# A plain 272-column v unit with the gates in it, and one gate preparation for prompt and sample, in a hybrid attention and mLSTM layer on one Trainium2 core

## The chip, the cores and the metric

The program runs on one core of one Trainium2 chip. Its time is the device time of that core in microseconds, from one execution to the next within some 0.1% here. TensorE is called PE in the profile (its weight loads PEld), VectorE DVE, ScalarE ACT, GpSimd POOL; SP is the engine whose queue issues most DMAs.

## What is computed

One encoder layer for a prompt of 1024 tokens and a sample of 256, with 2048 channels, all in float32. A normalised input is multiplied by one matrix of 9232 columns; its parts feed a neighbourhood attention of 8 heads and a two-way mLSTM of 4 heads, and their gated results go through an output matrix. Of the 9232 columns the last 16 are the mLSTM's gates.

```python
hn = rmsnorm(x, norm_w)
proj = jnp.einsum('btd,dp->btp', hn, w_in)
na_q, na_k, na_v, na_g, ml_qk, ml_v, ml_o, ml_z, ml_gp = jnp.split(proj, cuts, axis=-1)
att = neighbourhood_attention(na_q, na_k, na_v, na_rpb) * jax.nn.silu(na_g)
gates = ml_gp.reshape(B, T, 2, 2, ML_HEADS) + gate_b
log_i = gates[:, :, :, 0]
log_f = jax.nn.log_sigmoid(gates[:, :, :, 1])
...
mixed = jnp.concatenate([att, mem], axis=-1)
return x + jnp.einsum('btm,md->btd', mixed, w_out)
```

## The kernel before

**Numbers in two parts.** Every float32 operand of a large product is split into a high and a low part (`split`, lines 176 to 182, and `split_a`, 184 to 186): ACT rounds the source to the high part, DVE subtracts it from the source for the low part. A product then takes three matmuls: high by high, high by low, low by high (`mm_c`, lines 285 to 287).

**Two stages of projections.** The 1280 tokens (prompt, then sample) are cut into a first group of 768 (GA) and a second of 512 (GB). The first stage makes all columns for the first group, the second stage the same columns for the second group; then come attention and mLSTM units, interleaved, and the output product.

**A pair unit of the first stage** (`pair_a`, from line 484; its tiles are named A with the number of its first 128-column block) makes two blocks of 128 columns for 768 tokens. It treats the product as one of 2 x 2 blocks (column blocks by token halves of 384, contracted over two channel halves) and uses seven block products in place of eight. The sums of the input that this needs are made once, in `first_tiles` (lines 329 to 335), and are held in SBUF as `xb` and `xg` (`xop`, lines 279 to 283): with x(h, t) for channel half h and token half t, operand 1 is x(0,0), 2 is x(1,0), 3 is x(1,1), 7 is x(1,1) - x(0,1). The sums of weights are made on POOL per unit (line 536). Weights are stationary, 384 tokens are moving. For each of four row groups and each of seven products there are one split and six matmuls of 384 columns, 168 matmuls in all. Seven PSUM banks hold the products, three under the tag "pr" (three slots) and four under "a" (five slots). In the last row group DVE folds the banks into the two result tiles (`fold`, lines 501 to 521; additions at line 499, scaling at line 264), which lie in the five slots of "pc".

**What follows a unit** is a generator (`finish_a`, lines 439 to 482) that is stepped on inside the next unit: convolution for the mLSTM's q and k (blocks 24 to 39), storing k or q, a tanh and a store for the output gates (blocks 40 to 47). A v unit (block 56 and up) has its result transposed by PE, two 128 x 128 transposes for each of six token tiles (line 475), then split and stored (`store_v`, lines 234 to 248); tiles 1 and 3 use a "pc" slot for that, the others a single buffer "vo".

**The gates of the first group** (`gates_a`, lines 572 to 607) run behind the second unit (A6). The 16 columns' high and low weights stand side by side as 32 columns of a stationary operand, padded to 128 (tiles gAt), over the same input operands; 64 matmuls of 384 columns (gAb, line 596) make them, and twelve small matmuls (line 604) add high and low and turn them to token-major; DVE adds the bias (line 605) into `gt`.

**The order of units** is a list (lines 620 to 623): 4, 6, 24, 56, 8, 10, 26, 58, 12, 14 and so on, to 54. The loop at line 632 runs it.

**The second stage** begins at line 1475: `proj_v(4)` (token-major, x stationary, 272 columns moving, the gates' 16 among them; matmuls at line 774), the sums of squares, then the gate preparation `ml_gates` (lines 962 to 1088), first for the prompt and then for the sample, with high priority; then `proj_v(0)`, `proj_pair(0)`, and the units `pair_s` (tiles named S). `ml_gates` takes log f, makes running sums with five triangle or ones matrices on PE (line 988), transposes log f and i apart, one token tile at a time (line 1008), copies them out (1009), scans them on DVE in both directions (1015, 1017), and transposes back. The prompt and the sample each have their own scratch tile ("gm", two slots, one of which holds the triangles).

**The order on an engine** is not that of the text. The framework plans it with a model of the engines when the program is built: an instruction has a priority by its place in the text, or a higher one (`tc.high_priority()`), and is placed when its operands and a buffer slot are ready in the model. `tc.issue_after` pins an instruction behind another. On the chip each engine then keeps the planned order.

## Time and profile before

| | us |
|---|---|
| median of 3 runs | 2547.41 |
| lowest and highest | 2546.06, 2548.14 |
| the profiled execution, its own time | 2548.95 |
| its span, first to last instruction | 2547.2 |
| PE busy in the span | 2530.2 |
| DVE, ACT, POOL busy | 1979.9, 1348.7, 597.9 |
| the gates' matmuls of the first group, start to the next unit | 137.35 to 149.35 |
| unit A56 | 179.84 to 208.97 |
| gate preparation, first to last matmul | 1133.17 to 1190.59 |

A row of the profile names the line of the kernel, the engine, the operation, and the tiles written and read ("out<-in", buffer numbers left out). In a row of one tile or line the three figures are the shortest, median and longest duration in ns, then the first and the last start in us. A row of waits gives who waited for whom, the sum in us, the number of times and the longest. A row of the timeline gives start, length and the number of instructions merged. Matmuls overlap, so the distance of their starts and not their duration says how fast they go.

### The profile page before, as it was taken

What the parts mean: (1) busy time and instruction counts of PE and PEld (TensorE: products, weight loads), DVE (VectorE), ACT (ScalarE), POOL (GpSimd) and SP (SyncE); (2) the same over time, 40 slices, a digit from 0 to 9 for tenths busy, and PEclk for the clock granted to TensorE, in tenths of its full rate; (3) what the DMA queues carried; (4) which work ended last, traced back from release to release, by engine and by line L of the source; (5) the groups of instructions that cost most, each with busy time, mean ns of one, the idle gap of its engine ahead of it and who ended that gap; (6) DMA issues with size and microseconds to landing.
All of it is one profiled execution on the core that took longest, in us unless ns stands there. A gap on an engine that the chain in (4) does not pass through costs nothing.

```text
span 2547.2 us, 44847 instructions
## 1 busy us (share of the span) xinstructions
PE 2530.2 (99%) x15165; PEld 2370.7 (93%) x15165; DVE 1979.9 (78%) x4050; ACT 1348.7 (53%) x3053; POOL 597.9 (23%) x895
## 2 busy tenths in 40 slices
PE   9999999999999999999999999999999999999998
PEld 9999999999999999999999899899998888888887
DVE  8868788898969798988875676776775665889696
ACT  8635545444444444465655665666665553344445
POOL 0535555444444444410000011010100103000002
PEclk9999999999999999999999999999999999999999
DMA  6556474536434343476778878888877849646227
GB/s 217 164 159 204 137 231 129 182 120 194 131 112 127 108 129 100 135 245 211 232 247 272 267 267 288 273 261 266 298 230 240 291 126 352 204 145 212 90 87 256
DMA packets 307757, 505.67 MB, mean 199 GB/s; under 512 B 48992, under 2 KB 195080, under 8 KB 307528
## 3 DMA queue, kind: packets, MB, share of 16 engines
q1 hardware_dynamic: 304424, 490.75, 60.0%
q0 software_dynamic: 2960, 11.80, 1.2%
q8 instruction: 120, 1.97, 0.3%
q14 instruction: 109, 0.89, 0.1%
q10 hardware_dynamic: 144, 0.26, 0.0%
HBM read 374.18 MB, written 128.52 MB: 197 GB/s over the span
## 4 chain that ended last, share of the span: by engine, by line
PE 84%; DMA 2%; DVE 1%; issue 0%; ACT 0%; SPq 0%; POOLq 0%; POOL 0%; ACTq 0%; DVEq 0%
PE pc L691 16%; PE po L1681 15%; PE pv L774 6%; PE A40b L287 1%; PE A16b L287 1%; PE A52b L287 1%; PE A48b L287 1%; PE A44b L287 1%; PE A20b L287 1%; PE A42b L287 1%; PE A22b L287 1%; PE A14b L287 1%; PE A38b L287 1%; PE A50b L287 1%; PE A68b L287 1%; PE A46b L287 1%
## 5 line engine op out<-in xcount | busy, mean ns | idle before, releaser
L1681 PE MATMUL po<-wo,mo 128*128 128x512 f32 (+1 forms) x1620 | 374.2, 392 | 0.0
L1681 PEld LDWEIGHTS po<-wo,mo 128*128 128x128 f32 x1620 | 303.5, 188 | 70.0
L179 DVE TENSOR_TENSOR ws<-wr,ws 128x512 fp32r<-128x512 f32 x144 | 98.5, 693 | 38.4 <-ACT ws L178 37.9
L178 ACT CAST ws<-wr 128x512 fp32r<-128x512 f32 x144 | 87.6, 617 | 65.7 <-PE pc L691 58.0
L178 ACT CAST mo<-mb 128x640 fp32r<-128x640 f32 x72 | 52.0, 727 | 110.0 <-PE po L1681 99.5
L119 POOL TENSOR_SCALAR rs<-rs 128x1 f32<-128x1 f32 x9 | 4.2, 468 | 370.0 <-DVE rs L1634 366.9
L179 DVE TENSOR_TENSOR mo<-mb,mo 128x640 fp32r<-128x640 f32 x72 | 58.9, 826 | 30.8 <-ACT mo L178 30.8
L1602 DVE TENSOR_TENSOR y<-y,po 128x512 f32<-128x512 f32 x89 | 57.3, 685 | 13.9 <-PE po L1681 13.7
L178 ACT CAST mo<-ms 128x640 fp32r<-128x640 f32 x40 | 28.9, 725 | 51.2 <-PE po L1681 30.8
L179 DVE TENSOR_TENSOR wsv<-wr_v,wsv 128x512 fp32r<-128x512 f32 x64 | 44.3, 698 | 13.2 <-ACT wsv L178 13.0
L178 ACT CAST wsv<-wr_v 128x512 fp32r<-128x512 f32 x64 | 38.9, 616 | 23.7 <-PE pv L774 12.6
L429 DVE SCALAR_TENSOR_TENSOR pcv<-pco,cw_sb,pcv 128x516 f32<-128x516 f32 x48 | 36.8, 767 | 7.0 <-ACT pcv L423 7.0
L179 DVE TENSOR_TENSOR mo<-ms,mo 128x640 fp32r<-128x640 f32 x40 | 32.9, 821 | 10.0 <-ACT mo L178 10.0
L1616 ACT ACTIVATE jk<-y 128x512 f32<-128x512 f32 x39 | 24.5, 629 | 27.1 <-DVE y L1602 26.8
L1115 POOL MEMSET mls_0v<- 128x2 f32 x4 | 0.4, 101 | 160.4 <-DVE S_dt.float L179 136.9
L132 ACT ACTIVATE xq<-xq 128x1024 f32<-128x1024 f32 x20 | 21.2, 1061 | 31.4 <-DMA xq<-in_xtok_dram 29.0
L287 PE MATMUL fb<-xg,fw 128*128 128x384 f32 x192 | 34.7, 335 | 0.1
L287 PEld LDWEIGHTS fb<-xg,fw 128*128 128x128 f32 x192 | 33.3, 188 | 0.4 <-ACT xg L185 0.4
L1565 DVE TENSOR_TENSOR ms<-mb,mb 128x640 f32<-128x640 f32 x40 | 32.8, 821 | 0.0
L264 DVE TENSOR_TENSOR pco<-pc,rstdb 128x512 f32<-128x512 f32 x28 | 19.1, 687 | 16.6 <-PE pc L691 15.7
L812 DVE CUSTOM_DVE_ANT_0 nap_0st<-nap_0s,nap_0bt 128x384 f32<-128x384 f32 x32 | 17.7, 553 | 15.7 <-PE nap_0s L807 7.8
L815 ACT ACTIVATE nap_0st<-nap_0st,nap_0sm 128x384 f32<-128x384 f32 x32 | 19.7, 617 | 19.0 <-DVE nap_0sm L812 19.0
(2790 smaller groups left out, 8524.1 us busy)
## 6 DMA issues: line engine op xcount, KB each, us to landing
wr<-in_w_in_dram SPq DMA_DIRECT2D x72, 512.0 KB, 4.9
wr_v<-in_w_in_dram SPq DMA_DIRECT2D x32, 512.0 KB, 5.5
wb<-in_w_o_dram SPq DMA_DIRECT2D x48, 256.0 KB, 3.9
xq<-in_xtok_dram SPq DMA_DIRECT2D x20, 512.0 KB, 5.0
mb<-mx POOLq DMA_DIRECT2D x32, 320.0 KB, 7.9
y<-in_xtok_dram SPq DMA_DIRECT2D x35, 256.0 KB, 5.1
wr_wp<-in_w_o_dram SPq DMA_DIRECT2D x16, 512.0 KB, 6.2
vS<-vo SPq DMA_DIRECT2D x24, 256.0 KB, 5.1
```

Source lines behind the costliest of these rows:

```text
L132: S.activation(raw, raw, AF.Square, accum_out=ssq[g][:, t, q : q + 1])
L178: S.copy(hi, src)
L179: return V.tensor_tensor(lo, src, f(hi), op=ALU.subtract)
L287: PE.matmul(o, w(a_), x(b_), start=first and m == 0, stop=last and m == 2)
L429: V.scalar_tensor_tensor(dst[:, a:n], src[:, a + j - pad : n + j - pad], cw_sb[:, ct, j : j + 1], dst[:, a:n], op0=ALU.mult, op1=ALU.add,)
L691: PE.matmul(pb[j], t[j][:, wi, c : c + P], xs[xi], start=first and m == 0, stop=last and m == 2,)
L774: PE.matmul(outs[tt], xs[:, tt * P : (tt + 1) * P], t[:, wi, q * w : (q + 1) * w], start=first and m == 0 and (gates or tt % 2 == 0), stop ...
L815: S.activation(st, st, AF.Exp, bias=sm[:, 0:1], scale=-1.0, accum_out=sm[:, 2:3])
L1565: V.tensor_tensor(t, x, y_, op=op)
L1602: V.tensor_tensor(Y[p, q, tt], Y[p, q, tt], bk, op=op)
L1616: S.activation(jk, Y[p, q, tt], AF.Square, accum_out=ss[t][:, c : c + 1])
L1681: PE.matmul(bk[tt] if o is None else o, m[xi][:, tt * P : (tt + 1) * P], w[wi][:, cs], start=first and kk == 0 and j == 0, stop=last and j ...
```

## The change

`pair_a(56)` and `gates_a` go. In their place stands `unit_vg`, at the sixth place of the order, behind units 8 and 40, which move ahead of it. It makes the 256 v columns and the 16 gate columns together, token-major: the input operands 1, 2, 3 and 7 are stationary, 272 columns of weights are moving. The first token half is x(0,0) a + x(1,0) b, the second is x(1,1)(a + b) - (x(1,1) - x(0,1)) a, with a and b the two channel halves of the weights; eight products in place of seven and no folding afterwards. There are 8 steps of 4 products, 3 token tiles and 3 passes. Six banks hold the results, the three "a" banks those of the first half and the three "pr" banks those of the second. They are scaled, split and stored straight from PSUM, without transposes, and the gates are read from columns 256 to 271 of the same banks. Weights come from a new array, `w_vg`, laid out on the host.

`ml_gates` is cut in two: `ml_gates_all` does log f, the triangle products and the sums bd and bo once for all ten token tiles, and puts i and log f side by side into one tile `mgrw` of 40 columns; `ml_gates` keeps the scans for prompt and sample apart, and transposes both rows at once from `mgrw`.

```diff
--- before.py
+++ after.py
@@ -53,6 +53,7 @@
     xtok: bass.AP,
     w_in: bass.AP,
     w_g: bass.AP,
+    w_vg: bass.AP,
     w_o: bass.AP,
     lnw: bass.AP,
     rpb_tab: bass.AP,
@@ -481,6 +482,43 @@
                 store_v((n1 - NCH) // 2, tt * P, vo, b[:, :256])
                 yield
 
+    def unit_vg(bg):
+        banks = {(z, tt): bank("a" if z else "pr", f"vg{z}{tt}")[:, :272] for z in range(2) for tt in range(3)}
+        for kk in range(8):
+            raw = wa.tile([P, 1024], F32, tag="ra", name=f"vgr{kk}", bufs=NRA)
+            DM.dma_start(raw[:, :544], w_vg[kk])
+            a, b = raw[:, 0:272], raw[:, 272:544]
+            ab = raw[:, 544:816]
+            G.tensor_tensor(ab, a, b, op=ALU.add)
+            for i, z, src, scale in ((1, 0, a, None), (2, 0, b, None), (3, 1, ab, None), (7, 1, a, -1.0)):
+                t = wa.tile([P, GA], F32R, tag="pc", name=f"vgs{kk}{i}", bufs=NPC)
+                t = t[:, :544].rearrange("p (h c) -> p h c", h=2)
+                last_split["ins"] = split(t[:, 0], t[:, 1], src, scale).ins
+                for tt in range(3):
+                    for m, (xi, wi) in enumerate(((0, 0), (0, 1), (1, 0))):
+                        PE.matmul(
+                            banks[z, tt], xop(i, kk, xi)[:, tt * P : (tt + 1) * P], t[:, wi],
+                            start=kk == 0 and i in (1, 3) and m == 0,
+                            stop=kk == 7 and i in (2, 7) and m == 2,
+                        )
+                if i in (2, 7):
+                    next(bg, None)
+        for _ in bg:
+            pass
+        for z, tt in banks:
+            k = 3 * z + tt
+            rc = rcs[0][:, k : k + 1]
+            if k % 2:
+                vo = wa.tile([P, GA], F32R, tag="pc", name=f"vgo{k}", bufs=NPC)
+                vo = vo[:, :512].rearrange("p (a d) -> p a d", a=2)
+            else:
+                vo = wa.tile([P, 2, 256], F32R, tag="vo", name=f"vgo{k}", bufs=1)
+            store_v(0, k * P, vo, banks[z, tt][:, :256], rc)
+            V.scalar_tensor_tensor(
+                gt[:, k, :], banks[z, tt][:, 256:], rc, gb_sb, op0=ALU.mult, op1=ALU.add
+            )
+        return iter(())
+
     def pair_a(n1, bg=iter(()), hook=None, first=False, pinned=False):
         nm = f"A{n1}"
         tags = ("pr", "pr", "pr", "a", "a", "a", "a")
@@ -569,43 +607,6 @@
             pass
         return finish_a(n1, Cn)
 
-    def gates_a():
...
     opening = first_tiles()
     next(opening)
     cw_sb = const.tile([P, 16, 5], F32, tag="cw", name="cw_sb")
@@ -618,9 +619,10 @@
     DM.dma_start(w4_sb, mlnw)
     V.tensor_scalar(w4_sb, w4_sb, 0.25, None, op0=ALU.mult)
     order = [4, 6]
-    rest = list(range(KT0, QK0, 2)) + list(range(OT0, NCH, 2))
+    rest = [KT0, OT0, *range(KT0 + 2, QK0, 2), *range(OT0 + 2, NCH, 2)]
     for i in range(NU):
         order += [QK0 + 2 * i, NCH + 2 * i, *rest[2 * i : 2 * i + 2]]
+    order[3:6] = [KT0, OT0, NCH]
     pools = []
 
     def second_pools():
@@ -630,9 +632,10 @@
 
     bg = opening
     for i, n1 in enumerate(order):
-        bg = pair_a(n1, bg, second_pools if i == len(order) - 1 else None, i == 0, i == 1)
-        if i == 1:
-            gates_a()
+        if n1 == NCH:
+            bg = unit_vg(bg)
+        else:
+            bg = pair_a(n1, bg, second_pools if i == len(order) - 1 else None, i == 0, i == 1)
         k = i - 4
         if 0 <= k < 8:
             x_square(1, k)
@@ -959,34 +962,33 @@
             for i, (cm, base) in enumerate(((-1, 0), (1, 0), (1, -1), (-1, -1)))
         ]
 
-    def ml_gates(sq, tris):
-        nt, t0 = (2, 8) if sq == "s" else (8, 0)
-        T = nt * P
-        nm = f"mg{sq}"
-        ig = gt[:, t0 : t0 + nt, 0:8]
-        fg = gt[:, t0 : t0 + nt, 8:16]
+    def ml_gates_all(tris):
+        n = TT // P
+        ig, fg = gt[:, :, 0:8], gt[:, :, 8:16]
 
         def sm(name):
-            return late.tile([P, nt, 8], F32, tag=f"{nm}{name}", name=f"{nm}{name}")
-
-        bd, bo, em = (sm(n) for n in ("bd", "bo", "em"))
-        tmp = xs2.tile([P, 512], F32, tag="gm", name=f"{nm}tmp", bufs=2)
-        lf, e, PL, EX, tot, mc, a1, mF = (
-            tmp[:, i * nt * 8 : (i + 1) * nt * 8].rearrange("p (t c) -> p t c", c=8)
-            for i in range(8)
+            return late.tile([P, n, 8], F32, tag=f"mg{name}", name=f"mg{name}")
+
+        bd, bo, em = (sm(x) for x in ("bd", "bo", "em"))
+        tmp = xs2.tile([P, 512], F32, tag="gm", name="mgtmp", bufs=2)
+        e, PL, EX, tot = (
+            tmp[:, i * n * 8 : (i + 1) * n * 8].rearrange("p (t c) -> p t c", c=8) for i in range(4)
         )
-        mL = e
+        rw = po("mgrw")[:, : n * 40].rearrange("p (t c) -> p t c", c=40)
+        G.memset(rw, 0.0)
+        lf = tmp[:, 4 * n * 8 : 5 * n * 8].rearrange("p (t c) -> p t c", c=8)
         V.scalar_tensor_tensor(e, fg, -1.0, fg, op0=ALU.mult, op1=ALU.max)
         S.activation(e, e, AF.Exp, scale=-1.0)
         S.activation(e, e, AF.Ln, bias=1.0)
         V.tensor_scalar(lf, fg, 0.0, None, op0=ALU.min)
         V.tensor_tensor(lf, lf, e, op=ALU.subtract)
-        b = bank("a", f"{nm}tri")
-        n8 = nt * 8
+        V.tensor_copy(rw[:, :, 0:8], ig)
+        V.tensor_copy(rw[:, :, 32:40], lf)
+        b = bank("a", "mgtri")
         lf2 = lf.rearrange("p t c -> p (t c)")
         for i, m in enumerate((*tris, ones)):
-            PE.matmul(b[:, i * n8 : (i + 1) * n8], m, lf2, start=True, stop=True)
-        bv = b[:, : 5 * n8].rearrange("p (i t c) -> p i t c", i=5, c=8)
+            PE.matmul(b[:, i * n * 8 : (i + 1) * n * 8], m, lf2, start=True, stop=True)
+        bv = b[:, : 5 * n * 8].rearrange("p (i t c) -> p i t c", i=5, c=8)
         V.tensor_copy(PL[:, :, 0:4], bv[:, 0, :, 0:4])
         V.tensor_copy(PL[:, :, 4:8], bv[:, 1, :, 4:8])
         V.tensor_copy(EX[:, :, 0:4], bv[:, 2, :, 0:4])
@@ -994,20 +996,36 @@
         V.tensor_copy(tot, bv[:, 4])
         V.tensor_tensor(bd, ig, PL, op=ALU.subtract)
         V.tensor_tensor(bo, ig, EX, op=ALU.add)
-        rows = []
+        return tmp, (bd, bo, em, PL, tot, rw)
+
+    def ml_gates(sq, tmp, shared):
+        nt, t0 = (2, 8) if sq == "s" else (8, 0)
+        T = nt * P
+        nm = f"mg{sq}"
+        n8 = nt * 8
+        bd, bo, em, PL, tot, rw = (x[:, t0 : t0 + nt] for x in shared)
+
+        def sm(name):
+            return late.tile([P, nt, 8], F32, tag=f"{nm}{name}", name=f"{nm}{name}")
+
+        if sq == "p":
+            mL, mc, a1, mF = (
+                tmp[:, o : o + n8].rearrange("p (t c) -> p t c", c=8) for o in (320, 0, 384, 448)
+            )
+        else:
+            mc, a1 = sm("mc"), sm("a1")
         rfi, rma = (
             [xs2.tile([8, TP], F32, tag="gr", name=f"{nm}r{w_}{i}", bufs=4) for i in range(2)]
             for w_ in "im"
         )
-        for r_, (w_, src) in enumerate((("f", lf), ("i", ig))):
-            r = rfi[r_]
-            for c in range(0, nt, 4):
-                b = bank("a", f"{nm}{w_}{c}")
-                cn = min(4, nt - c)
-                for t in range(cn):
-                    PE.transpose(b[0:8, t * P : (t + 1) * P], src[:, c + t, :], ident)
-                V.tensor_copy(r[:, c * P : (c + cn) * P], b[0:8, : cn * P])
-            rows.append(r[:, :T])
+        for c in range(0, nt, 4):
+            b = bank("a", f"{nm}r{c}")
+            cn = min(4, nt - c)
+            for t in range(cn):
+                PE.transpose(b[0:40, t * P : (t + 1) * P], rw[:, c + t, :], ident)
+            for r, o in zip(rfi, (32, 0)):
+                V.tensor_copy(r[:, c * P : (c + cn) * P], b[o : o + 8, : cn * P])
+        rows = [r[:, :T] for r in rfi]
         b = bank("a", f"{nm}mc")
         for d in range(2):
             mr = rma[d][:, :T]
@@ -1475,8 +1493,8 @@
     proj_v(4, X)
     x_stats(1, lambda c: po(f"xdg1_{c}")[:, :256])
     with tc.high_priority():
-        tris = ml_tris()
-        gates = {sq: ml_gates(sq, tris) for sq in ("p", "s")}
+        shared = ml_gates_all(ml_tris())
+        gates = {sq: ml_gates(sq, *shared) for sq in ("p", "s")}
     proj_v(0, X)
     proj_pair(QT0, X)
     operand_sums()
@@ -1795,6 +1813,8 @@
     w_g = np.ascontiguousarray(
         cols["gp"][:, gorder].reshape(KT, P, 16).transpose(1, 0, 2).reshape(P, KT * 16)
     )
+    wv = np.concatenate([cols["v"][:, :256], cols["gp"][:, gorder]], axis=1)
+    w_vg = np.ascontiguousarray(wv.reshape(2, 8, P, 272).transpose(1, 2, 0, 3).reshape(8, P, 544))
     w_o = np.ascontiguousarray(
         g["w_out"][0].reshape(KT, P, 4, 512).transpose(2, 1, 0, 3).reshape(4, P, KT * 512)
     )
@@ -1826,6 +1846,7 @@
         "xtok": np.ascontiguousarray(x),
         "w_in": w_in,
         "w_g": w_g,
+        "w_vg": w_vg,
         "w_o": w_o,
         "lnw": np.ascontiguousarray(g["ln_w"][0].reshape(KT, P).T),
         "rpb_tab": tab,
```

More of the change, by code (lines that the diff above doesn't have):

```diff
@@ L570, in pair_a @@
         return finish_a(n1, Cn)
-    def gates_a():
-        raw = wa.tile([P, 1024], F32, tag="ra", name="gAw", bufs=NRA)
-        DM.dma_start(raw[:, :256], w_g)
-        ab = [raw[:, :P], raw[:, P : 2 * P]]
-        ext = [raw[:, 256 : 256 + P], raw[:, 384 : 384 + P]]
-        V.tensor_tensor(ext[0], ab[0], ab[1], op=ALU.add)
-        V.tensor_scalar(ext[1], ab[0], -1.0, None, op0=ALU.mult)
-        st = []
-        for i, src in enumerate((*ab, *ext)):
-            t = wsa(f"gAt{i}").rearrange("p h c -> p (h c)")[:, : 8 * 32 + 96]
-            G.memset(f(t), 0.0)
-            tv = t[:, :256].rearrange("p (k h c) -> p k h c", h=2, c=16)
-            sv = src.rearrange("p (k c) -> p k c", c=16)
-            split_a(tv[:, :, 0, :], tv[:, :, 1, :], sv)
-            st.append(t)
-        sel = raw[0:32, 512:528]
-        V.tensor_tensor(sel, ident[0:32, 0:16], ident[0:32, 16:32], op=ALU.add)
-        gs = pc("gAg")
-        for th, prods in enumerate((((0, 1), (1, 2)), ((2, 3), (3, 7)))):
-            b = bank("a", f"gAb{th}")[:, :HALF]
-            n = 0
-            for w_, i in prods:
-                for kk in range(8):
-                    for hl_ in range(2):
-                        PE.matmul(
-                            b, st[w_][:, kk * 32 : kk * 32 + P], xop(i, kk, hl_),
-                            start=n == 0, stop=n == 31,
-                        )
-                        n += 1
-            V.tensor_copy(gs[0:32, th * HALF : (th + 1) * HALF], b[0:32])
-        for tt in range(GA // P):
-            b = bank("a", f"gAt{tt}")
-            PE.matmul(b[:, :16], gs[0:32, tt * P : (tt + 1) * P], sel, start=True, stop=True)
-            V.scalar_tensor_tensor(
-                gt[:, tt, :], b[:, :16], rcs[0][:, tt : tt + 1], gb_sb, op0=ALU.mult, op1=ALU.add
-            )
     opening = first_tiles()
```

## The prediction

> **What bounds the kernel now.** I read the page first: busy time by engine, the row of the granted clock, and the chain of work that ended last.

> ```profile
> PE 2530.2 (99%) x15165; PEld 2370.7 (93%) x15165; DVE 1979.9 (78%) x4050; ACT 1348.7 (53%) x3053; POOL 597.9 (23%) x895
> ...
> PEclk9999999999999999999999999999999999999999
> ...
> PE 84%; DMA 2%; DVE 1%; issue 0%; ACT 0%; SPq 0%; POOLq 0%; POOL 0%; ACTq 0%; DVEq 0%
> ```

> The reader is to see that PE is busy for 2530.2 of 2547.2 us at one clock throughout, and that the chain runs through it; no other engine is above 78%. Next, whom PE waited for, over the whole span (11 rows, 8.8 us in all; the longest, the one beside the edited place, the last):

> ```profile
> PE fb L287 <- ACT fw L185: 1.7, 1, 1.7
> ...
> PE A6b L287 <- DVE A4c L499: 0.4, 1, 0.4
> ...
> PE A4b L287 <- DVE A4s L186: 0.3, 1, 0.3
> ```

> So there are no stalls worth removing. Time is won only by giving PE less to issue, and lost only by stalls or slower matmuls. A busy PE says nothing of the pace, so the third view is a table of stretches that I cut at the boundaries of units: A6, the gates' block, A24, A56, A8, then the 272-wide v unit of the second stage, and the two places of the gate preparation.

> ```profile
> core 0: us, PE busy (x) PEld busy (x) DVE busy (x) ACT busy (x) POOL busy (x), PEclk, DMA share, GB/s
> 107.50:137.35 29.85, 29.48 (x170) 29.06 (x170) 27.11 (x57) 17.37 (x43) 16.49 (x19) 1.00 0.73 215
> 137.35:149.35 12.00, 12.00 (x72) 11.72 (x71) 7.93 (x19) 3.69 (x9) 2.41 (x4) 1.00 0.51 150
> 149.35:179.84 30.49, 30.49 (x176) 30.21 (x175) 17.25 (x40) 11.36 (x28) 11.05 (x15) 1.00 0.45 138
> 179.84:208.97 29.13, 29.13 (x170) 29.13 (x170) 28.84 (x46) 15.21 (x35) 15.07 (x15) 1.00 0.41 118
> 208.97:239.20 30.23, 30.23 (x178) 29.89 (x178) 24.27 (x51) 13.91 (x38) 14.32 (x18) 1.00 0.68 203
> ...
> 1095.35:1107.33 11.98, 11.98 (x97) 11.98 (x97) 10.97 (x20) 6.95 (x13) 0.91 (x5) 1.00 0.68 232
> 1133.17:1135.99 2.82, 2.82 (x29) 2.49 (x28) 2.56 (x6) 2.78 (x6) 0.00 (x0) 1.00 0.25 102
> 1178.41:1179.88 1.47, 1.47 (x17) 1.40 (x16) 1.29 (x3) 1.18 (x3) 0.13 (x2) 1.00 1.18 347
> ```

> A count is one or two high where a matmul straddles a cut. A pair unit issues 168 matmuls (4 row groups, 7 products, 2 halves, 3 passes), so A56 gives **29.13 / 168 = 0.1734 us per 384-wide matmul**. The sixth data row holds 96 matmuls of 272 columns: **11.98 / 96 = 0.1248 us each**. These differences of starts are the price of a matmul; the duration in a row is not, since neighbours overlap:

> ```profile
> L774 PEld LDWEIGHTS pv<-wsv,x_0h x64: 187/188/192, 1095.2 to 1836.3; 128*128 128x128 f32 x64
> L774 PE MATMUL pv<-wsv,x_0h x64: 274/282/386, 1095.4 to 1836.4; 128*128 128x256 f32 x56, 128*128 128x272 f32 x8
> ```

> **The change, part by part.** First what PE loses. The timeline around the gates:

> ```profile
> 137.35 2.95 PE L596 MATMUL gAb<-xb,gAt 128*128 128x384 f32 x16
> 140.13 8.52 PE L596 MATMUL gAb<-xg,gAt 128*128 128x384 f32 x48
> 148.58 0.84 PE L604 MATMUL gAt<-gAw,gAg 32*128 32x16 f32 x6
> 149.35 1.32 PE L287 MATMUL A24b<-xb,A24s 128*128 128x384 f32 x6
> ...
> 152.90 0.84 PE L604 MATMUL gAt<-gAw,gAg 32*128 32x16 f32 x6
> 153.67 2.38 PE L287 MATMUL A24b<-xg,A24s 128*128 128x384 f32 x12
> ```

> The 64 gate matmuls and half of the gAt ones take 137.35 to 149.35 = 12.00 us; the other half, inside A24, takes 153.67 - 152.90 = 0.77. A56 takes 29.13. Its twelve transposes ride in A8 and A10: in A8's stretch ten of them add 30.23 - 29.13 = 1.10, 0.11 each, 1.32 in all. Removed: 12.00 + 0.77 + 29.13 + 1.32 = **43.22 us**.

> What PE gains: unit_vg issues 8 x 4 x 3 x 3 = 288 matmuls, x stationary and 272 columns moving, the form of the sixth row: 288 x 0.1248 = **35.94 us**. Net in the first stage: -7.28. A24's stretch also holds 30.49 - 29.13 - 0.77 = 0.59 us that no matmul explains; I leave it in and count it only in the low end.

> Then the gate preparation:

> ```profile
> 1133.17 1.00 PE L988 MATMUL mgptri<-mgptmp,tris 128*128 128x64 f32 x8
> 1134.01 0.39 PE L988 MATMUL mgptri<-mgptmp,ones 128*128 128x64 f32 x2
> 1134.23 1.04 PE L1008 MATMUL mgpf<-ident,mgptmp 128*8 128x128 f32 x8
> 1135.11 1.04 PE L1008 MATMUL mgpi<-ident,gt 128*8 128x128 f32 x8
> ...
> 1178.41 0.96 PE L988 MATMUL mgstri<-mgstmp,tris 128*128 128x16 f32 x8
> 1179.22 0.38 PE L988 MATMUL mgstri<-mgstmp,ones 128*128 128x16 f32 x2
> 1179.44 0.38 PE L1008 MATMUL mgsf<-ident,mgstmp 128*8 128x128 f32 x2
> 1179.66 0.38 PE L1008 MATMUL mgsi<-ident,gt 128*8 128x128 f32 x2
> ```

> The ten prompt passes take 1134.23 - 1133.17 = 1.06, the ten sample passes 1179.44 - 1178.41 = 1.03, so 16 columns cost what 64 cost and 80 in common will cost about 1.1: 1.03 goes. Transposing f and i as one 40-wide row block halves 16 + 4 transposes at 0.11: 1.10 goes. Together **-2.13**. All stand between matmuls of proj_v and pair_s on a PE that does not idle, so they count in full. Sum: -7.28 - 2.13 = **-9.41 us**.

> **What is hidden, and by what.** A split on ACT and DVE, the evictions with a scale, the gates' eviction, and the stores of the v tiles, with the one time (2.7 us) that ACT stood still for such a store; the last row is one of the two scans of the sample's chain:

> ```profile
> L185 ACT CAST A26s<-A26t x16: 402/407/432, 263.1 to 289.8; 128x256 fp32r<-128x256 f32 x16
> L186 DVE TENSOR_TENSOR A26s<-A26t,A26s x16: 412/424/989, 263.5 to 290.3; 128x256 fp32r<-128x256 f32 x16
> L181 ACT ACTIVATE vo<-pv,rstdc x32: 454/471/510, 1120.3 to 1874.7; 128x256 fp32r<-128x256 f32 x32
> L182 DVE SCALAR_TENSOR_TENSOR vo<-pv,rstdc,vo x32: 462/476/486, 1122.7 to 1875.9; 128x256 fp32r<-128x256 f32 x32
> L787 DVE SCALAR_TENSOR_TENSOR gt<-pv,rstdc,gb_sb x4: 230/232/234, 1123.1 to 1126.4; 128x16 f32<-128x16 f32 x4
> L248 SPq DMA_DIRECT2D vS<-A56vo x12: 451/547/1849, 223.4 to 245.2; - x12
> ...
>   DMA vS<-A56vo: 2.7, 1
> ...
> DMA to landing us min/median/max: 2.5/3.9/5.5
> ...
> L1015 DVE TENSOR_TENSOR_SCAN mgsrm<-mgsri,mgsri x1: 679/679/679, 1182.0 to 1182.0; 8x256 f32<-8x256 f32 x1
> ```

> unit_vg needs 32 splits (scaled by 272/256, about 0.45 on DVE and 0.43 on ACT), each feeding nine matmuls, 1.12 us; a pair's split feeds six, 1.04 us. Evictions: 6 x (0.476 + 0.232) = 4.2 on DVE. DVE has some 18.6 us of its own in 36, less than the 28.84 of 29.13 that A56's stretch carried with A24's convolution beside it and no PE wait. That convolution now rides beside A8, a unit of the same shape. POOL has 8 additions in place of 16; SP loads eight pieces of 272 KB in place of four of 512 and the gates' 64. Cost of all this on PE: none while the splits run ahead.

> Three seams can bite. At A6 to A24 the gates' 12 us of PE cover goes while DVE was busy 27.11 of A6's 29.85 us; A4 to A6, the nearest row, cost 0.4. At the start of unit_vg three "a" banks are wanted at once, of which A40 frees two during its last folds: bounds 0 and two DVE operations such as those above, 0.9. At its end all three "pr" banks are its own, and the next unit starts on them: a bank is free after 0.471 + 0.476, but the first "pr" bank closes six matmuls (0.75 us) before the unit ends, and two "a" banks stand free for other products; bounds 0 and 0.95. I take 0.4 and 0.5, together **+0.9**, near the 0.4 of the observed seam.

> Forecast: -9.41 + 0.9 = **-8.5 us**. The profiled execution took 2548.95 (span 2547.2 and 1.75 around it), which becomes 2540.4; it lies 1.5 above the median of the runs, 2547.41, so the median becomes **2538.9**.

> **Rivals.** *A stall at the end of unit_vg.* The even output tiles share one buffer ("vo", bufs=1), so the third and fifth eviction each wait for the store before. By the rows a link is 0.95 of eviction, two issues at 0.547 and 3.9 to 5.5 to land; two links and the last eviction give 13 to 16 us, counted from about 2 us before the unit's end, and the fifth tile is a "pr" bank. The next unit reaches its third "pr" product 2.1 us in. Were PE's order fixed there, PE would idle 9 to 12 us: 2548 to 2551, no gain left. Against it: the engines' orders are planned and not those of the text, five other products can go first, and in A56v the same chain held ACT for 2.7 us and PE not at all. I give it 10%. [...]

> *The common preparation comes at a bad time.* The sample's chain waited for the prompt's scratch tile; now it may press its DVE work (two scans at 0.68 and some eight copies and small operations, by my estimate 3 us) in among the splits of proj_v and proj_pair, where DVE was busy 2.56 of 2.82. If no split is ahead, PE gives 3 us back: 2542. For it, high priority; against, the prompt's longer chain cost nothing. 15%.

> *Slower: splits too late.* In unit_vg each split takes one of five "pc" slots, which A40's two result tiles and three output tiles share. If slots run out, PE waits for the chain ACT to DVE each time: 0.43 + 0.45 by 32 = 28 us, so 2567. It turns the sign from (9.4 + 5.1) / 32 = 0.45 us a split. Against: three slots are left at worst, 3.4 us of matmuls over a chain of 0.9, and A40's tiles leave after two activations and a store. 4%.

> *Slower: weight loads set the pace.* If the 0.188 us of a load were the interval, unit_vg would take 288 x 0.188 = 54.1, 18.2 more: 2557; it turns the sign above 0.175 us a matmul. Against it stand 96 such loads in 11.98 us. 2%. [...]

> **How the numbers follow.** Forecast 69%, its own range 2536.4 to 2540.8: the low end takes the 0.59 back and sets the seams to nothing (2537.4), the high end doubles the seams (2539.8), and 1 us either way is the runs' scatter. The rivals hold 10, 15, 4 and 2%. The 8-in-10 range is **2535.5 to 2545**, through the second rival and short of the first. A measurement here tells about 0.2% from no change, 5.1 us: faster means below 2542.3. Faster: 69 and about half of the second rival, 77%; same: the rest of that and most of the first, 17%; slower: 6%.

> **What would show it.** In the profile after: about 36 us for the unit's 288 matmuls with a pace of 0.125; no gate block behind A6; PE waits beside unit_vg's ends below 1 us; one set of ten tri passes; the busy sum of PE down by about 9. I am wrong if the pace is above 0.13, if PE waits several us for a bank of the unit, or if new waits stand in stages that the diff doesn't touch.

## The result and the profile after

The changed kernel takes **2542.95 us** (median of 18 runs, 2541.19 to 2549.05) beside 2548.02 for the kernel before (18 runs, 2546.06 to 2551.17). The ratio is 0.9983, 95% interval [0.9976, 0.9989]: faster, by 0.17%, which is less than the 0.2% named beforehand as what a measurement can tell from no change; by the prediction's own line of 2542.3 the result counts as "same", which had 17%. The forecast of -8.5 us became -5.1. The 8-in-10 range holds the time; the likeliest case's own range, up to 2540.8, doesn't.

The profiled execution took 2542.98, a span of 2541.2. From its page:

```profile
PE 2521.8 (99%) x15177; PEld 2362.5 (93%) x15177; DVE 1982.5 (78%) x4026; ACT 1346.7 (53%) x3048; POOL 595.3 (23%) x884
...
PEclk9999999999999999999999999999999999999999
...
PE 86%; DMA 3%; DVE 2%; ACT 1%; issue 1%; SPq 0%; POOLq 0%; POOL 0%; ACTq 0%; DVEq 0%
```

PE is still the bound, 99% busy at a mean granted clock of 0.999 (0.999 before as well), and its busy sum fell by 8.4 us where 9.4 were to go. But the span fell by 6.0, and in the chain DVE's share went from 1% to 2%. The list of PE's waits (us in total, times, longest) says where:

```profile
PE A26b L288 <- DVE gt L517: 1.8, 2, 1.6
PE pc L694 <- DVE ws L180: 1.8, 1, 1.8
...
PE pc L694 <- ACT ws L179: 0.3, 1, 0.3
```

The first two waits are new, and both are for DVE. The table of stretches, cut at the first matmuls of A6, A24, A40, the joint unit, A26 and A58:

```profile
core 0: us, PE busy (x) PEld busy (x) DVE busy (x) ACT busy (x) POOL busy (x), PEclk, DMA share, GB/s
106.20:136.05 29.85, 29.48 (x170) 29.06 (x169) 28.36 (x53) 17.59 (x43) 14.79 (x16) 1.00 0.78 229
136.05:165.15 29.10, 29.10 (x170) 29.10 (x169) 24.11 (x45) 13.21 (x33) 13.93 (x17) 1.00 0.67 217
...
194.37:223.96 29.59, 29.38 (x170) 29.05 (x168) 24.97 (x46) 13.06 (x33) 13.98 (x14) 1.00 0.46 145
223.96:260.00 36.04, 36.04 (x290) 36.04 (x289) 20.80 (x43) 18.06 (x44) 8.35 (x11) 1.00 0.34 107
260.00:291.69 31.69, 29.87 (x171) 29.26 (x170) 21.91 (x47) 12.45 (x34) 13.93 (x18) 1.00 0.53 148
```

The joint unit takes 36.04 us for its 288 matmuls, 0.125 each, as worked out. The unit behind it, A26, takes 31.69 where one takes 29.1, with PE idle for 1.8 of it. One more stretch changed, the eight S units of the second stage, which the diff doesn't touch (first the kernel before, then after):

```profile
1194.30:1348.70 154.40, 154.40 (x1346) 1.00 0.75 236
```

```profile
1187.50:1342.80 155.30, 155.30 (x1346) 1.00 0.74 235
```

As many matmuls, no idle time in either, and 0.9 us more: each matmul starts 115.6 ns after the last instead of 114.9. In one table (from the first matmuls of A6, of the first projection of values, of the first and the last S unit and of the output product; "unit alone" to "both, pinned, old addresses" are runs told below):

| us | before | after | unit alone | prep. alone | both, pinned | unit, pinned | both, pinned, old addresses | the same, copies on ACT |
|---|---|---|---|---|---|---|---|---|
| opening, to A6 | 107.5 | 106.2 | 107.3 | 106.3 | 107.4 | 105.6 | 106.6 | 106.8 |
| first stage from A6 | 987.9 | 982.5 | 981.9 | 987.9 | 980.3 | 980.2 | 980.0 | 980.0 |
| of it, A26 | 29.1 | 31.7 | 31.2 | 29.1 | 29.1 | 29.2 | 29.1 | 29.1 |
| values and q, k of the second stage, with the gate preparation | 98.9 | 98.8 | 99.2 | 96.9 | 98.0 | 98.9 | 98.0 | 96.5 |
| S units to the last | 154.4 | 155.3 | 154.4 | 155.4 | 155.4 | 154.4 | 154.5 | 154.5 |
| last S unit, attention, mLSTM | 801.4 | 801.8 | 800.4 | 799.9 | 804.0 | 800.4 | 799.3 | 804.1 |
| output product | 397.1 | 396.6 | 397.1 | 396.7 | 396.6 | 397.0 | 397.1 | 397.0 |
| span | 2547.2 | 2541.2 | 2540.3 | 2543.1 | 2541.7 | 2536.5 | 2535.5 | 2538.9 |

Each column is one execution. Most rows that concern the change repeat within 0.1 to 0.7 us between kernels that share the part in question. The preparation's stage does so with the old preparation (98.8 to 99.5 in six profiles) and not with the common one as it stands (96.9 to 100.2 in six, by how long PE waits in it and, in the longest, by a granted clock of 0.5 for 3.4 us). PE's busy time in it is steadier: 98.0 to 98.4 with the old preparation, 95.9 to 96.4 with the common one (97.4 in the execution with the slow clock). The opening (105.6 to 107.6 over all fourteen profiles) and the attention (799.3 to 804.1, with waits of up to 2.5 us for loads of q and k) scatter as well, so single spans are not compared below; stages are.

### The profile page after: what moved, and what is told of

The parts are those of the page before. It is cut to its first block, busy times and chain, and to the rows that moved or that the text cites. A ratio compares the mean times of both kernels' runs of the same rounds, so it can differ in the third digit from the quotient of the medians.

```text
span 2541.2 us, 44814 instructions
## 1 busy us (share of the span) xinstructions
PE 2521.8 (99%) x15177; PEld 2362.5 (93%) x15177; DVE 1982.5 (78%) x4026; ACT 1346.7 (53%) x3048; POOL 595.3 (23%) x884
## 4 chain that ended last, share of the span: by engine, by line
PE 86%; DMA 3%; DVE 2%; ACT 1%; issue 1%; SPq 0%; POOLq 0%; POOL 0%; ACTq 0%; DVEq 0%
PE pc L694 15%; PE po L1699 15%; PE pv L777 4%; PE A22b L288 1%; PE A10b L288 1%; PE A44b L288 1%; PE A14b L288 1%; PE A48b L288 1%; PE A18b L288 1%; PE A52b L288 1%; PE A46b L288 1%; PE A20b L288 1%; PE A12b L288 1%; PE A70b L288 1%; PE A38b L288 1%; PE A50b L288 1%
```

## The experiments

The theory after the result had three parts. D: at the joint unit's end DVE comes late to the evictions, since splits of the next unit stand ahead of them. P: the common preparation does save PE its 2.1 us, but PE then arrives at the projection before DVE has got through the scans. M: the S units are longer because something moved in SBUF, not because of work. The rival at the unit's end was V, the chain of stores through the single buffer "vo", which the prediction had as its first rival.

### The two changes apart

```diff
-        shared = ml_gates_all(ml_tris())
-        gates = {sq: ml_gates(sq, *shared) for sq in ("p", "s")}
+        tris = ml_tris()
+        gates = {sq: ml_gates(sq, tris) for sq in ("p", "s")}
```

That edit of the kernel after, with the old `ml_gates`, is the unit alone; the same edit the other way round, made to the kernel before, is the preparation alone.

> unit_vg and the new order of units stay, the gate preparation is that of before. Theory P (the common preparation gives back what it saves, because DVE there is late with the splits of proj_pair): the time is that of the changed kernel, 5 us under the kernel before, and PE's 1.8 us wait for DVE's ws in proj_pair is gone. Rival Q (the preparation keeps its 2.13 us and the loss is elsewhere): about 3 us under the kernel before, that is 2 us above the changed kernel.

> The kernel before with only the common gate preparation. Theory P: within 1 us of the kernel before, with a new PE wait of 1 to 2 us for ws in proj_pair. Rival Q: 2.1 us under the kernel before and no such wait.

The unit alone: 2540.57 us (6 runs), ratio to before 0.9968 [0.9956, 0.9980]. The preparation alone: 2547.21 (11 runs), ratio 0.9997 [0.9988, 1.0006]. So the unit earns what there is, and the preparation nothing that can be measured. For the unit alone that is better than either side expected: 7.5 us below before, and 2.4 below the median of the changed kernel. The table shows why the preparation earns so little: alone, it makes its own stage 2.0 shorter, and the S units 1.0 longer. The 1.0 that is left is inside the interval. The new wait for "ws" is there, but only 0.7 and 0.3 us long: P's cause takes 1.0 of the gain here, and the S units as much. With the unit alone the S units stay at 154.4, and A26 has its loss (31.2) all the same.

### The end of the joint unit

What DVE did there in the kernel after, then POOL, then PE (start and length in us):

```profile
258.63 0.96 DVE L187 TENSOR_TENSOR A26s<-A26t,A26s 128x256 fp32r<-128x256 f32 x1
259.51 0.41 DVE L187 TENSOR_TENSOR A26s<-A26r,A26s 128x256 fp32r<-128x256 f32 x1
259.85 0.95 DVE L187 TENSOR_TENSOR A26s<-A26t,A26s 128x256 fp32r<-128x256 f32 x1
260.73 0.41 DVE L187 TENSOR_TENSOR A26s<-A26r,A26s 128x256 fp32r<-128x256 f32 x1
261.06 0.94 DVE L187 TENSOR_TENSOR A26s<-A26t,A26s 128x256 fp32r<-128x256 f32 x1
261.93 0.41 DVE L187 TENSOR_TENSOR A26s<-A26r,A26s 128x256 fp32r<-128x256 f32 x1
262.26 0.47 DVE L183 SCALAR_TENSOR_TENSOR vgo<-vg,rstdc,vgo 128x256 fp32r<-128x256 f32 x1
262.66 0.22 DVE L517 SCALAR_TENSOR_TENSOR gt<-vg,rstdc,gb_sb 128x16 f32<-128x16 f32 x1
```

```profile
258.36 0.94 POOL L574 TENSOR_TENSOR A26t<-A26r 128x256 f32<-128x256 f32 x1
259.73 0.79 POOL L574 TENSOR_TENSOR A26t<-A26t,A26r 128x256 f32<-128x256 f32 x1 [0.43 <-DVE A26s L187]
260.88 0.84 POOL L574 TENSOR_TENSOR A26t<-A26r 128x256 f32<-128x256 f32 x1 [0.36 <-DVE A26s L187]
262.15 0.78 POOL L574 TENSOR_TENSOR A26t<-A26r,A26t 128x256 f32<-128x256 f32 x1 [0.43 <-DVE A26s L187]
```

```profile
260.00 1.38 PE L288 MATMUL A26b<-xg,A26s 128*128 128x384 f32 x7
263.02 1.29 PE L288 MATMUL A26b<-xb,A26s 128*128 128x384 f32 x6 [1.64 <-DVE gt L517]
```

The last matmul of the joint unit goes out just ahead of 260.00, and ACT has rounded four of the six outputs by 260.7. DVE's first eviction starts at 262.26, behind six splits of A26 that the planned order puts in front; PE has used the free banks by 261.4 and waits. The median split of A26 took 0.424 in the kernel before; here every second one takes 0.94 to 0.96, and those are the ones that start while POOL adds.

Two runs tell D from V. The first holds four of the splits back behind the second eviction:

```diff
+                late_ = n1 == QK0 + 2 and r == 0 and i not in (1, 5, 6)
+                with tc.issue_after(evicted[1]) if late_ else ExitStack():
-                split_a(t[:, 0], t[:, 1], src[i])
+                    split_a(t[:, 0], t[:, 1], src[i])
```

The second keeps DVE's order and gives every output tile but the first a "pc" slot, so that no output waits for a store:

```diff
-            if k % 2:
+            if k:
```

> The changed kernel, with four splits of the unit after unit_vg (its first row group, the products behind the first three) pinned on DVE behind the second eviction of unit_vg. Theory D (PE's loss of 2.56 us at the start of A26 is DVE's: nine splits of A26, slowed beside POOL's additions, stand ahead of the first eviction): A26's stretch falls from 31.69 to about 30.0 us and PE's wait for gt from 1.8 to under 0.4. Rival V (the single buffer vo makes the loss): 31.7 as it was, since the stores still hold ACT for 8 us.

> The changed kernel, with all output tiles of unit_vg but the first in slots of pc, so that no eviction waits for a store in vo; DVE's planned order has the first evictions where it had them. Theory D: A26's stretch falls by 0.5 us only, from 31.69 to 31.2, and the 1.6 us wait stays. Rival V: it falls to about 29.3, and ACT's waits of 5.8 and 2.3 us for the stores go with it.

With the splits held back, A26 takes 29.1 us, PE without a gap:

```profile
259.74 0.95 DVE L187 TENSOR_TENSOR A26s<-A26t,A26s 128x256 fp32r<-128x256 f32 x1
260.62 0.41 DVE L187 TENSOR_TENSOR A26s<-A26r,A26s 128x256 fp32r<-128x256 f32 x1
260.95 0.47 DVE L183 SCALAR_TENSOR_TENSOR vgo<-vg,rstdc,vgo 128x256 fp32r<-128x256 f32 x1
261.35 0.22 DVE L519 SCALAR_TENSOR_TENSOR gt<-vg,rstdc,gb_sb 128x16 f32<-128x16 f32 x1
```

```profile
261.30:290.40 29.10, 29.10 (x170) 29.10 (x169) 20.80 (x47) 12.37 (x34) 14.14 (x18) 1.00 0.57 161
```

With free slots, ACT's wait for the stores is gone (in the kernel after it is the first row below; no such row is left), and PE's wait stays as it was (second row); A26 takes 31.1:

```profile
ACT vgo L182 <- DMA vS<-vgo: 8.1, 2, 5.8
```

```profile
PE A26b L288 <- DVE gt L517: 1.6, 1, 1.6
```

D holds, and the repair is worth 2.6 us where 1.7 were expected. V accounts for at most 0.6 of the 2.6 us, and for less, since other runs with the chain in place have 30.9 to 31.3 for A26. The whole kernels: 2541.17 (11 runs; ratio 0.9972 [0.9963, 0.9981]) with the splits held back, 2542.39 (8 runs; 0.9972 [0.9962, 0.9982]) with free slots. Over whole kernels the two can't be told apart; the stage tells them.

### Why the S units are longer

The common preparation keeps two small results of the sample in the pool ahead of the x tiles. That pool grows by 128 bytes per partition, and what is allocated behind it moves by as much: the tiles x_12 to x_15, x_6 and x_7, and the S units' sums and half of their split weights. First the kernel after with those two results in a dead part of the scratch tile:

```diff
-            mc, a1 = sm("mc"), sm("a1")
+            mc, a1 = (tmp[:, o : o + n8].rearrange("p (t c) -> p t c", c=8) for o in (160, 176))
```

then the unit alone with the old preparation and 128 bytes of padding that nobody reads, and later the same with 256 bytes (`[P, 64]`) and pinned splits:

```diff
+    G.memset(late.tile([P, 32], F32, tag="pad", name="pad"), 0.0)
```

> The kernel after, with the sample's two small results of the gate preparation kept in a dead part of the common scratch tile, so that the pool ahead of the x tiles has its old size of 4672 bytes per partition and the x tiles lie at their old addresses (8288 and on instead of 8416). Theory M (the eight S units are 0.93 us longer because tiles x_7 and x_12 to x_15 lie at other addresses): the S units take 154.4 us again, the matmuls on x_12 to x_15 start 113 to 114 ns apart. Rival K (the common preparation itself slows them): 155.3 and 117 to 120 ns as in the kernel after. The wait for DVE's split at the entry of the projection (1.8 and 1) stays by both.

> The joint unit alone with the old gate preparation (as in the run of the unit alone), and 128 bytes per partition of unused padding in the pool ahead of the x tiles. Theory M: the S units take 155.3 us instead of 154.4, with 117 to 120 ns on x_12 to x_15. Rival K: 154.4, since the preparation is the old one.

> The joint unit with the old preparation and the pinned splits, with 256 bytes of padding per partition ahead of the x tiles in place of none. If the pace of the S units' matmuls goes with the address by a period of 256 bytes or less, 154.4 us as without padding; if with a period of 512 or more, another length, 153 to 156.

The S units' stretch in the three, in that order:

```profile
1190.00:1344.50 154.50, 154.50 (x1347) 1.00 0.74 236
```

```profile
1188.30:1343.70 155.40, 155.40 (x1347) 1.00 0.75 234
```

```profile
1186.60:1341.10 154.50, 154.50 (x1347) 1.00 0.74 235
```

M holds both ways: old addresses with the new preparation give the old length, padding with the old preparation gives the new one. 256 bytes give the old length again, as a pace that repeats every 256 bytes would; no other shift was run. In the kernel after, which has the 128 bytes, the matmuls on the high parts of x_12 to x_15 start 116.0 to 118.6 ns behind the matmul ahead of them (means of a tile) and in the kernel before 113.4 to 114.1, while those on the high part of x_1 go from 121.3 to 117.5; x_1 itself didn't move, so it isn't the address of the moving operand alone. The output product shows the opposite sign, 396.6 or 396.7 with the shift and 397.0 or 397.1 without it in all fourteen profiles. Why the pace changes no run shows. One run of each: 2546.11, 2545.31 and 2540.02, beside 2549.14 for the kernel before.

### The wait at the projection

DVE in the kernel after, with the splits "ws" that the projection needs:

```profile
1136.32 0.67 DVE L180 TENSOR_TENSOR ws<-wr,ws 128x512 fp32r<-128x512 f32 x1
...
1137.86 2.27 DVE L1033 TENSOR_TENSOR_SCAN mgprm<-mgpri,mgpri 8x1024 f32<-8x1024 f32 x1
1140.06 2.25 DVE L1035 TENSOR_TENSOR_SCAN mgprm<-mgpri,mgpri 8x1024 f32<-8x1024 f32 x1
...
1142.66 0.67 DVE L180 TENSOR_TENSOR ws<-wr,ws 128x512 fp32r<-128x512 f32 x1
...
1144.20 0.67 DVE L180 TENSOR_TENSOR ws<-wr,ws 128x512 fp32r<-128x512 f32 x1
```

PE enters the projection at 1138.89 and waits at 1143.10 to 1144.92 for the last of these. In the kernel before, PE entered at 1147.81, and the scans stand so:

```profile
1144.03 2.27 DVE L1015 TENSOR_TENSOR_SCAN mgprm<-mgpri,mgpri 8x1024 f32<-8x1024 f32 x1
1146.23 2.25 DVE L1017 TENSOR_TENSOR_SCAN mgprm<-mgpri,mgpri 8x1024 f32<-8x1024 f32 x1
```

Then PE came 0.7 us ahead of their end, now it comes 3.4 ahead. PE's part of the preparation got shorter and DVE's didn't: the four row copies of 0.67 to 0.68 and the two scans stand in both. The wait itself varies: 1.8 and 0.3 us here, 1.0 to 1.9 in sum in the five other profiles with the common preparation in this place. Two runs move DVE's part. In one the preparation is handed over behind the projection and the operand sums:

```diff
-    with tc.high_priority():
-        shared = ml_gates_all(ml_tris())
-        gates = {sq: ml_gates(sq, *shared) for sq in ("p", "s")}
     proj_v(0, X)
     proj_pair(QT0, X)
     operand_sums()
+    with tc.high_priority():
+        shared = ml_gates_all(ml_tris())
+        gates = {sq: ml_gates(sq, *shared) for sq in ("p", "s")}
```

In the other, which also has the pinned splits and the old addresses, the row copies are ACT's:

```diff
-                V.tensor_copy(r[:, c * P : (c + cn) * P], b[o : o + 8, : cn * P])
+                S.copy(r[:, c * P : (c + cn) * P], b[o : o + 8, : cn * P])
```

> The kernel after with its gate preparation handed over later, behind the projection of the queries and the sums of the operands and not ahead of them. Theory P (the preparation's scans stand on DVE in the way of the splits that the projection waits for): the wait of 1.8 + 0.3 us at the entry of the projection goes, from the first projection of the values to the first S unit 96.7 to 97.2 us instead of 98.8, the kernel 2541. Rival Q (DVE is short of time there in any order): the wait comes back at another place ahead of or in the S units, and 2543 stays.

> Both changes, with the four splits held behind the second eviction, the x tiles at their old addresses, and the copies of the transposed gate rows (four of 0.69 us for the prompt, two for the sample) on ACT and not on DVE. ACT stands idle from 1133.9 to 1137.0 there in the kernel after; the two scans then start some 2.7 us earlier on DVE. Theory P (DVE's scans stand in the way of the projection's splits, since PE arrives sooner and DVE's chain has grown no shorter): the wait of 1.8 and of 0.3 goes, from the first projection of the values to the first S unit 96.7 instead of 98.8, and the kernel 2 us below the run without this edit: 2538. Rival Q (DVE is short of time there in any order): the wait moves to the first split, now behind the scans, 1 to 2 us, and the kernel stays within 0.5 of the other.

Handing it over later was a miss for both theories; Q had the place, but not the size: 2552.44 us (10 runs), 1.0018 [1.0008, 1.0028] of before, slower. The wait at the projection is gone, but the preparation's own steps now stand in PE's order behind nothing that covers them:

```profile
PE mgsmc L1039 <- DVE mgsrm L1033: 3.6, 1, 3.6
PE mgsmc L1039 <- DVE mgsmc L1042: 2.2, 1, 2.2
PE mgpmp L1074 <- DVE mgtmp L1075: 2.2, 1, 2.2
```

The clock adds to it: from 1188.3 to 1198.5 the granted clock is 0.5, beginning right behind the first of these waits in time, one of 2.2 us, and reaching into the first S unit, whose matmuls on x_1 to x_3 last 415 ns and not 279 to 288 as in the kernel after; the S units take 156.7.

With the copies on ACT the scans come ahead of the first split and are over before PE enters at 1137.9:

```profile
1131.22 2.27 DVE L1037 TENSOR_TENSOR_SCAN mgprm<-mgpri,mgpri 8x1024 f32<-8x1024 f32 x1
1133.42 2.25 DVE L1039 TENSOR_TENSOR_SCAN mgprm<-mgpri,mgpri 8x1024 f32<-8x1024 f32 x1
1135.60 0.65 DVE L180 TENSOR_TENSOR ws<-wr,ws 128x512 fp32r<-128x512 f32 x1
```

In that stage 0.2 us of waits are left, and it takes 96.5 us, 2.4 below before, 1.9 of it in PE's busy time: P holds for the stage, and here stands the gain that was forecast.

### The repaired kernels together

> The joint unit with the old gate preparation, and four splits of the next unit held behind the second eviction of the joint unit, as in the run with pinned evictions. If the terms add, the next unit takes 29.1 us, the S units 154.4, and the kernel is 1.8 below the unit alone (2540.6): 2538.8, about the time that was forecast for both changes together. If the 1.6 us are given back in the first stage or in the attention, 2540 to 2541.

> Both changes, with the four splits held behind the second eviction and the x tiles at their old addresses, the copies on DVE as in the kernel after. Next unit 29.1, S units 154.4, the wait of 1.8 + 0.3 at the entry of the projection stays: 2540.2 by the run with pinned evictions alone (2541.2) less 0.93. Against the unit alone with pinned evictions it tells what the common preparation is worth here: nothing or a loss of up to 1 us if the wait takes its whole gain, 2 us better if not.

> The joint unit with the old preparation and the pinned splits once more, on the chip of the two runs beside it, so that the three can be compared: 2539 if that result holds (0.9964 of before); by theory P 1 us above the run with the copies on ACT and 1 us below the one without.

The joint unit alone with pinned splits (the first edit and the pin) took 2539.08 (5 runs; 0.9964 [0.9952, 0.9976]), and 2539.06 the second time (5 runs; 0.9959 [0.9946, 0.9971]). Beside that second run stood both changes with the pin and the old addresses, 2538.05 (5 runs; 0.9958 [0.9946, 0.9971]), and the same with the copies on ACT, 2539.23 (5 runs; 0.9959 [0.9945, 0.9972]). All are some 10 us below the kernel before, and can't be told apart. The copies on ACT were expected 2 us below the run beside it and are 1.2 above, though their stage is 1.5 shorter; and the three came out in the reverse of the expected order. The profile with the copies on ACT has 4.8 us more in the attention. Of these, 2.8 are idle time of PE (3.8 against 1.0; its longest waits are 2.0 and 0.8 for loads of q and k and 0.8 for DVE), and 2.0 are busy time, most of it from a granted clock of 0.5 from 1642.7 to 1646.1, right behind the longest wait. The load with that wait was waited for 1.6 and 0.3 us in the two profiles of the joint unit alone with pinned splits, which is one kernel, so such a wait scatters; and the two profiles compared are the slowest of the one kernel's five runs (2540.63) and the fastest of the other's (2537.22). Whether the edit plays a part stays open, and with it what the common preparation is worth to the whole kernel.

## Why the prediction was right or wrong

The direction was right, and so was the mechanism of the gain, less for PE to issue. What the seams and the preparation would cost was wrong, and with it the size. Two of the prediction's own signs of being wrong came: PE waits 1.6 us at the joint unit's end, where less than 1 was to show, and a new wait stands at a projection that the diff doesn't touch. From profile to profile the span fell by 6.0: opening -1.3 (chance), first stage -5.4, preparation's stage -0.1, S units +0.9, attention +0.4, output product -0.5.

- **What goes and what comes, -7.28: right.** From A6 to A24, 41.85 - 29.85 = 12.00 went, and the unit cost 36.04 against 35.94. The twelve transposes were worth 1.5 and not 1.32: of two units behind a v unit the first takes 30.4 and the second 29.35, against 29.13 elsewhere. A24's unexplained 0.59, left out of the forecast, went as well: 30.5 became 29.1. So did 0.7 us that A12 took before beyond the 30.4 of its place, 0.3 of it a wait; no run shows why.
- **The seams, +0.9: the failed step in the first stage.** A6 to A24 cost nothing that shows, and neither did the entry of the unit; A40 ahead of it takes 0.5 more than 29.1, but for a split of its own in its middle, at 209.63. The end cost 2.6, where the bounds were 0 and 0.95. Those bounds took an eviction to start as soon as its bank closes. In the kernel after DVE first worked through six splits planned ahead of it, every second one at 0.95 us beside POOL, and the eviction started at 262.26. The kernel before had that 0.95 in a row quoted in the prediction (a median of 424 ns, a longest of 989) and I read only the median.
- **The stall at the unit's end, 10%: the wrong chain.** ACT did wait 8.1 us for stores, and PE hardly cared. It and the bounds of both ends of the unit were also argued on swapped banks: the code gives the "pr" banks to the first token half and the "a" banks to the second; the prediction and the description ahead of it have it the other way round. The output tiles in "pr" banks are therefore the first three, of which only the third stands behind a store, and the last of them closes 18 matmuls, 2.25 us, before the unit ends in the order of the code: the loss by the banks alone was, by that estimate, nearer 0.
- **The preparation, -2.13: right on PE, lost twice.** The step "on a PE that does not idle, so they count in full" failed. In the profile of the kernel after, 2.1 us come back as a wait for splits behind DVE's scans (1.0 to 1.9 in the others), and 0.9 go in the S units; the 15% rival had this mechanism and its place, but named the sample's scans of 0.68 and not the prompt's of 2.27. Its 2542 is the nearest of all to the measured time, and half by accident: the loss behind the unit is of the same size.
- **The S units, +0.93: not thought of.** The prediction counted what each instruction costs, and not that two new small tiles move what is allocated behind them by 128 bytes.
- **Slots and weight loads:** neither rival showed. 288 matmuls at 0.125 us, with weight loads of 0.188 each, refute the loads as pace here.

The forecast as a ratio, 2538.9 / 2547.41 = 0.9967, is about what the joint unit alone reaches once the next unit's splits are pinned (0.9964 and 0.9959). That is chance: this kernel has neither the preparation's 2.13 nor the seams' 0.9 in it.

## What to carry to other kernels

When work is taken from the engine that bounds, look at each place where it now arrives earlier, and ask which engine was only just ahead there: both losses here were DVE's, at places without a wait before. For an eviction, ask what the planned order puts ahead of it, not when its bank closes, and use the longest duration in the row if the neighbour engine is at work (here 0.95 us for a split beside POOL's additions, 0.41 between them). And compare the pace of stages that a diff doesn't touch: two new tiles of 128 bytes together cost 0.9 us here, nearly what ten saved transposes bring (1.10).

## What the runs showed of the hardware

**A DVE operation with two inputs in SBUF beside a POOL addition.** In the rows above, the splits that start within a POOL addition take 0.94 to 0.96 us and end 0.28 to 0.29 us after it, those that start in POOL's pauses 0.41. In the whole first stage of that kernel, the 508 splits of the A units that start outside a POOL addition take 0.407 to 0.430, whatever tile they read; of the 416 that start within one, 391 take longer, up to 1.02, and of the 311 that take over 0.6, 310 end 0.28 to 0.30 us after the addition. The eviction at 262.26, which reads PSUM, starts within one too and takes its 0.47.

**The pace of the S units' matmuls (float32, 256 columns) changed with where tiles lie**: 114.9 ns from start to start over 1344 of them, 115.6 with 128 bytes of padding, 115.0 with 256. The runs don't show why.
